# Three unused pieces of on-chip memory that move the start addresses of the weights, the features and the gated values

## The chip, the cores and the metric

The kernel runs on one core of a Trainium2 chip. The time is the device time of one execution in microseconds (us), the median of several runs. One run was also profiled. Everything is float32; the large products use the float32r kind of the matrix engine, with each operand split into a high and a low part.

## The reference, cut to what matters

Two transformer blocks over 512 tokens of width 1024 (528 tokens in the first block, with 16 meta tokens ahead):

```python
# first block, h is (528, 1024)
h = h + 0.5 * (silu(n1(h) @ w_gate1) * (n1(h) @ w_up1)) @ w_down1      # d_ff 2816
u = rmsnorm(h) ; parts = split(u @ w_in)                                # 20 + 16 blocks of 128 columns
y = sigmoid(g1) * (mla(parts) @ w_mla_o) + sigmoid(g2) * (gated_deltanet(parts) @ w_gdn_o)
h = h + y @ w_out
h = h + 0.5 * (silu(n2(h) @ w_gate2) * (n2(h) @ w_up2)) @ w_down2
x = rmsnorm(h)[16:]                                                     # (512, 1024)
# second block
shift, scale, gate = split(silu(c) @ w_ada + b_ada)
p = (rms_norm(x) * (1 + scale) + shift) @ w_in_2                        # q, k, v, gates
o = concat(banded_attention(p) * silu(z_a), (cmp + sel + win attention)(p) * silu(z_b))
out = x + gate * (o @ w_out_2)
```

## The kernel before

Everything lies transposed: 128 features on the partitions, tokens along the free dimension. A product sums over K blocks of 128 features. For each block the matrix engine (PE) makes three matmuls, because a product of split operands is high by high, high by low and low by high. The stationary operand (`lhsT`, loaded by a LDWEIGHTS that the profile shows as PEld) is a 128 by 128 piece of weights, and the moving operand (`rhs`) is a slice of features, 512 columns wide in most of the program and 272 and 256 columns (two halves of 528 tokens) in the first feed-forward layer and the projections after it. The loop that does most of it is in `mm_steps`, and its matmul is line 348:

```python
for a, x, first, last in ((wh, 0, c == 0, False), (wh, 1, False, False), (wl, 0, False, c == K - 1)):
    for i, (b, hl) in enumerate(zip(banks, xs)):
        T.matmul(b[:, :hl[x].shape[2]], lhsT=a[:, kk], rhs=hl[x][:, c], ...)
```

So the names of a row read like this: `b<-xh,whi` is a matmul into bank b with moving operand `xh` (features, high part) and stationary operand `whi` (weights, high part).

Weights come as raw pieces of 1024 columns (`wraw`) by DMA from SyncE's queue. `split_weights` halves each into two pieces of up to 512 columns, ScalarE (ACT, line 307) writes the high part and VectorE (DVE, line 308) the low part. A piece goes to one of three buffers `whi` and `wlo` in the pool `weights`, and every fourth piece to the extra buffers `whix` and `wlox`, which lie in a different pool at another place:

```python
more = extra[0] is not None and made[0] % (HALF + 1) == 0        # HALF = 3
hi, lo = [extra[0].tile([128, HW], F32R, tag=t + "x", ...) if more else
          wp.tile([128, HW], F32R, tag=t, ..., bufs=HALF) for t in ("whi", "wlo")]
```

A piece of 512 columns is four K blocks, so it feeds 12 matmuls of 512 moving columns, or 12 pairs of 272 and 256.

Pools are stacked from the left and from the right end of each partition's memory, tile after tile, in the order in which the program opens them. From the left stand first the pool `const` (the tiles `cst` of 2148 bytes and `vec` of 808 bytes), then `weights`, `big`, `small`, and then what a stage needs. From the right stand the features `xh0`, `xl0` (272 tokens) and `xh1`, `xl1` (256 tokens), later `xh2`, `xl2` and `h2`, and the three extra weight pools one after another (`weights_x1` in the first layer and the projections, `weights_x2` in the second feed-forward layer, `weights_x3`, from the left, in the second block's projections). So one small tile early in a pool shifts everything stacked behind it. The small tile `mod` (24 values, line 1345) stands at the bottom of the left side during the second feed-forward layer and the second block.

The program's stages, in order of time: the first feed-forward layer (`gh`, `gl` are its gated values), the input projections, the delta rule and latent attention (many small float32 matmuls, with projections woven in), the merge with the product `wo` (`mh`, `ml` are its moving operand), the second feed-forward layer, the second block's projections by tokens (`tok_group`, lines 1552 to 1554, in which features are the stationary and weights the moving operand), its attention, and the output product.

The order of the instructions is that of the program's text; generators are woven by hand with fixed rates (`weave`, `braid`), and nothing in it depends on an address.

Of the kernel before, what the change touches and what calls it, by code (L numbers as in the profile page):

```python
# [9 lines left out]
F32 = mybir.dt.float32  # L10
# [207 lines left out]
def body(tc, A, out, VAT, CAT):  # L218
# [4 lines left out]
    def pool(name, bufs=1, side="left", st=es, **k):  # L223
        return st.enter_context(tc.tile_pool(name=name, bufs=bufs, side=side, **k))
# [4 lines left out]
        return st  # L229

    const = pool("const")
    psum = pool("psum", 1, space=PSUM)
    dram = pool("dram", 1, space=DRAM)
    wp = pool("weights")
# [1107 lines left out]
    ast = scope()  # L1342
    apl = pool("ada", side="right", st=ast)
    mdp = pool("mod")
    mod = mdp.tile([128, 24], F32, name="mod")
    csil = apl.tile([128, D], F32, name="csil")
    ct = apl.tile([128, D], F32, tag="wada", name="ct", bufs=3)
    SY.dma_start(out=ct, in_=A["crow"])
# [641 lines left out]
```

## Time and profile before

| what | value |
|---|---|
| median of three runs | 1579.91 us (1579.36 to 1581.45) |
| time of the profiled execution | 1572.62 us |
| its span, first to last instruction | 1570.8 us |
| mean granted clock of PE | 0.998 |
| PE busy | 1540.9 us, 98% of the span, 10214 matmuls |
| VectorE busy | 995.9 us, 63% |
| ScalarE busy | 637.2 us, 41% |
| DMA | 178.69 MB, mean 114 GB/s |

The ends of matmuls are modelled and successive ones overlap, so the spacing of a stream of matmuls is read from the starts of its rows, not from the durations.

### The profile page before, as it was taken

The page shows a single profiled execution, that of the slowest core. Times are in us where ns is not written, and L with a number is a line of the kernel's source. Part 1 is how long each engine was busy: PE and PEld are TensorE (multiplying, and loading weights), DVE is VectorE, ACT ScalarE, POOL GpSimd, SP SyncE. Part 2 cuts the span into 40 slices and gives each one's busy share as a digit, 9 for nine tenths or more (in the row PEclk, how much of TensorE's full clock was granted, in tenths as well). Part 3 has the DMA queues.
Part 4 walks back from the last instruction along what each step waited for, and adds up shares of the span by engine and source line. Part 5 has one row for each costly group of instructions (what it writes and reads, how often), then busy time and mean ns, then how long its engine had stood idle before and what let it go on. Part 6 is the DMA issues. An engine that isn't in the chain of part 4 may idle for free.

```text
span 1570.8 us, 26635 instructions
## 1 busy us (share of the span) xinstructions
PE 1540.9 (98%) x10214; PEld 1347.4 (86%) x10214; DVE 995.9 (63%) x2338; ACT 637.2 (41%) x1303; POOL 167.3 (11%) x233
## 2 busy tenths in 40 slices
PE   8999999999999989998999999999999999999999
PEld 8999999999999888997777888888888978877667
DVE  6554345545788788656657697434554786669963
ACT  6332233334324333235554333323333564448741
POOL 0000000000001311012210000000000140125530
PEclk9999999999999999999999999999999999999999
DMA  5322333234424354325125584233332545522014
GB/s 179 94 93 74 100 96 95 91 88 129 137 83 125 105 152 130 106 83 180 35 81 165 201 276 136 80 99 106 95 91 81 150 140 176 175 84 53 11 37 139
DMA packets 94672, 178.69 MB, mean 114 GB/s; under 512 B 16608, under 2 KB 43808, under 8 KB 94544
## 3 DMA queue, kind: packets, MB, share of 16 engines
q1 hardware_dynamic: 93392, 174.89, 36.5%
q10 hardware_dynamic: 1152, 2.10, 0.4%
q8 instruction: 80, 1.31, 0.4%
q14 instruction: 48, 0.39, 0.1%
HBM read 159.80 MB, written 16.11 MB: 112 GB/s over the span
## 4 chain that ended last, share of the span: by engine, by line
PE 89%; DVE 5%; DMA 2%; POOL 1%; ACT 1%; issue 1%; SPq 0%; DVEq 0%; ACTq 0%; POOLq 0%
PE b L348 68%; PE b L1934 2%; PE b L1554 1%; PE b L1552 1%; PE b L1553 1%; PE b L521 1%; PE b L330 1%; PE b L1915 1%; PE b L332 1%; PE b L331 1%; PE b L1248 1%; PE b L1228 1%; DVE pr L960 1%; DVE wlo L308 1%; PE b L1838 1%
## 5 line engine op out<-in xcount | busy, mean ns | idle before, releaser
L307 ACT ACTIVATE whi<-wraw 128x512 fp32r<-128x512 f32 (+3 forms) x414 | 242.1, 587 | 484.6 <-PE b L348 433.0
L348 PE MATMUL b<-xh,whi 128*128 128x256 f32 (+2 forms) x1428 | 374.1, 319 | 0.4 <-DVE tv L372 0.4
L308 DVE TENSOR_TENSOR wlo<-wraw,whi 128x512 fp32r<-128x512 f32 (+3 forms) x414 | 263.5, 639 | 168.3 <-ACT whi L307 165.3
L348 PE MATMUL b<-xl,whi 128*128 128x256 f32 (+2 forms) x1428 | 369.4, 316 | 0.0
L348 PE MATMUL b<-xh,wlo 128*128 128x256 f32 (+2 forms) x1428 | 369.4, 316 | 0.0
L348 PEld LDWEIGHTS b<-xh,whi 128*128 128x128 f32 x1428 | 234.3, 189 | 21.3 <-issue 0.9
L348 PEld LDWEIGHTS b<-xh,wlo 128*128 128x128 f32 x1428 | 234.9, 189 | 18.8 <-issue 0.4
L348 PEld LDWEIGHTS b<-xl,whi 128*128 128x128 f32 x1428 | 234.4, 189 | 18.1 <-issue 0.4
L348 PE MATMUL b<-gh,wlo 128*128 128x256 f32 (+2 forms) x446 | 114.8, 310 | 0.0
L348 PE MATMUL b<-gh,whi 128*128 128x256 f32 (+2 forms) x446 | 114.8, 310 | 0.0
L348 PE MATMUL b<-gl,whi 128*128 128x256 f32 (+2 forms) x446 | 114.6, 309 | 0.0
L307 ACT ACTIVATE whix<-wraw 128x512 fp32r<-128x512 f32 (+4 forms) x109 | 61.8, 567 | 128.1 <-PE b L348 113.4
L308 DVE TENSOR_TENSOR wlox<-wraw,whix 128x512 fp32r<-128x512 f32 (+4 forms) x109 | 66.5, 610 | 53.3 <-ACT whix L307 53.0
L348 PE MATMUL b<-xh,whix 128*128 128x272 f32 (+2 forms) x308 | 82.5, 321 | 0.0
L348 PE MATMUL b<-xh,wlox 128*128 128x272 f32 (+2 forms) x308 | 81.7, 319 | 0.0
L348 PE MATMUL b<-xl,whix 128*128 128x272 f32 (+2 forms) x308 | 81.7, 318 | 0.0
L348 PEld LDWEIGHTS b<-gl,whi 128*128 128x128 f32 x446 | 73.8, 188 | 4.8
L348 PEld LDWEIGHTS b<-gh,wlo 128*128 128x128 f32 x446 | 73.8, 188 | 4.7
L348 PEld LDWEIGHTS b<-gh,whi 128*128 128x128 f32 x446 | 73.8, 188 | 4.8
L457 DVE TENSOR_TENSOR g<-b,R 128x272 f32<-128x272 f32 (+2 forms) x66 | 32.5, 516 | 61.1 <-PE b L348 58.7
L460 DVE TENSOR_TENSOR u<-b,R 128x272 f32<-128x272 f32 (+1 forms) x66 | 32.1, 515 | 59.7 <-PE b L348 59.7
L348 PEld LDWEIGHTS b<-xh,whix 128*128 128x128 f32 x308 | 51.0, 188 | 4.6 <-issue 0.5
(495 smaller groups left out, 2666.2 us busy)
## 6 DMA issues: line engine op xcount, KB each, us to landing
wraw<-in_wgu_dram SPq DMA_DIRECT2D x85, 512.0 KB, 3.6
wraw<-in_win_dram SPq DMA_DIRECT2D x36, 512.0 KB, 3.6
wraw<-in_wdn_dram SPq DMA_DIRECT2D x35, 384.0 KB, 3.5
wada<-in_wada_dram SPq DMA_DIRECT2D x24, 512.0 KB, 4.9
wraw<-in_wdn_dram SPq DMA_DIRECT2D x35, 320.0 KB, 2.9
wraw<-in_wo_dram SPq DMA_DIRECT2D x17, 512.0 KB, 3.6
wraw<-in_w2t_dram SPq DMA_DIRECT2D x16, 512.0 KB, 4.2
wraw<-in_w2f_dram SPq DMA_DIRECT2D x10, 512.0 KB
```

Source lines behind the costliest of these rows:

```text
L307: SC.activation(hi[:, :w], raw, AF.Copy)
L308: V.tensor_sub(lo[:, :w], raw, hi[:, :w].bitcast(F32))
L330: T.matmul(ps, lhsT=wh, rhs=xh, start=start, stop=False)
L331: T.matmul(ps, lhsT=wh, rhs=xl, start=False, stop=False)
L332: T.matmul(ps, lhsT=wl, rhs=xh, start=False, stop=stop)
L348: T.matmul(b[:, :hl[x].shape[2]], lhsT=a[:, kk], rhs=hl[x][:, c], start=first and not (one and i), stop=last and (i > 0 or not one))
L457: V.tensor_mul(g[:, o:o + w], b[:, :w], R[:, o:o + w])
L460: V.tensor_mul(u[:, o:o + w], b[:, :w], R[:, o:o + w])
L521: T.matmul(pp[2 * i + a][:, :n_], lhsT=w[j], rhs=X[a][x][:, k], start=first, stop=last)
L960: V.tensor_tensor(out=t, in0=x[:m, 0:i, 0:i], in1=g[:m, 0:i, i].unsqueeze(1).to_broadcast([m, i, i]), op=ALU.mult)
L1228: T.transpose(p[:, o:o + 128], d["pn"][par][:, i, NM + j * 128:NM + j * 128 + 128], ident)
L1934: T.matmul(po[rs[par], j * 128:], lhsT=vt[:, j, g * 64:g * 64 + 64], rhs=Pt[par][:, o:o + S - j * 128], start=False, stop=br == 1 and j == 3)
```

## The change

Three pieces are allocated that nothing reads or writes: 48 values (192 bytes) in the pool `const`, ahead of `cst` and `vec`; 56 values (224 bytes) at the right edge, ahead of every pool of the right side; and `mod` gets 32 places in place of 24 (32 bytes more), of which the first 24 are used.

```diff
     const = pool("const")
+
+    const.tile([128, 48], F32, name="pad")
+    pool("edge", side="right").tile([128, 56], F32, name="edge")
     psum = pool("psum", 1, space=PSUM)
...
     mdp = pool("mod")
-    mod = mdp.tile([128, 24], F32, name="mod")
+    mod = mdp.tile([128, 32], F32, name="mod")[:, 0:24]
```

On each of the five engines the same instructions stand in the same order, with the same shapes and the same waits; line numbers behind the edit are three higher. What differs is where tiles start. These are the starts in the built programs, in bytes of a partition, as the remainder of a division by 256:

| tiles | before | after |
|---|---|---|
| `wraw` (3), `whi` (3), `wlo` (3) | 64 | 0 |
| `whix`, `wlox` of `weights_x1` and `weights_x2` | 224 | 0 |
| `whix`, `wlox` of `weights_x3` | 32 | 0 |
| `xh0`, `xl0` (slices of 1088 bytes), `xh1`, `xl1` (1024 bytes) | 224 | 0 |
| `gh` / `gl` of the first layer (slices of 2112 bytes) | 64 / 0 | 0 / 192 |
| `gh`, `gl` of the second layer (2048 bytes) | 32 | 0 |
| `xh2`, `xl2`, `h2` (2048 bytes) | 224 | 0 |
| `mh`, `ml`, `ogh`, `ogl` (2048 bytes) | 64 | 0 |
| `wada`, `csil` | 224 | 0 |
| `hT` | 64 | 0 |
| `pna`, `pnb`, `xt` | 224 | 192 |
| `cst`, `accq` | 128 | 64 |

A K block of weights is 512 bytes and a slice of `xh2` 2048 bytes, so the remainder of a tile's start holds for all of its slices; only the slices of 1088 and 2112 bytes step on by 64 from one to the next.

## Rows read from the trace of the kernel before

**Rows 1.** The page's first part: busy time and share by engine.
```profile
PE 1540.9 (98%) x10214; PEld 1347.4 (86%) x10214; DVE 995.9 (63%) x2338; ACT 637.2 (41%) x1303; POOL 167.3 (11%) x233
```

**Rows 2.** The chain that ended last, by engine.
```profile
PE 89%; DVE 5%; DMA 2%; POOL 1%; ACT 1%; issue 1%; SPq 0%; DVEq 0%; ACTq 0%; POOLq 0%
```

**Rows 3.** Stretches: length, busy us (count) of PE, PEld, DVE, ACT, POOL; clock; DMA.
```profile
30.00:405.00 375.00, 375.00 (x3078) 374.78 (x3078) 188.61 (x359) 125.56 (x219) 2.63 (x9) 1.00 0.33 98
...
900.00:1250.00 350.00, 350.00 (x1591) 286.52 (x1590) 201.16 (x344) 122.91 (x216) 1.73 (x5) 1.00 0.40 123
1250.00:1420.00 170.00, 166.47 (x859) 136.88 (x858) 121.56 (x270) 88.50 (x192) 44.55 (x52) 1.00 0.48 147
```

**Rows 4.** PE's longest wait: us in total, times, longest.
```profile
PE b L521 <- ACT whi L307: 5.6, 1, 5.6
```

**Rows 5.** Groups of matmuls by line and shape: count, busy us, mean ns.
```profile
L348 PE MATMUL b<-xh,whi 128*128 128x256 f32 x704 | 175.3, 288 | 0.0
L348 PE MATMUL b<-xh,whi 128*128 128x512 f32 x388 | 154.6, 399 | 0.0
L348 PE MATMUL b<-xh,whi 128*128 128x272 f32 x336 | 97.6, 291 | 0.4 <-DVE tv L372 0.4
L348 PE MATMUL b<-gh,whi 128*128 128x512 f32 x104 | 41.1, 395 | 0.0
L1552 PE MATMUL b<-whi,xh 128*128 128x512 f32 x72 | 28.7, 401 | 0.0
```

**Rows 6.** Timeline of PE in the second feed-forward layer: start us, us.
```profile
943.07 0.40 PE L348 MATMUL b<-xh,whi 128*128 128x512 f32 x1
...
945.88 0.40 PE L348 MATMUL b<-xh,whix 128*128 128x512 f32 x1
...
946.81 0.39 PE L348 MATMUL b<-xl,whix 128*128 128x512 f32 x1
...
948.62 0.39 PE L348 MATMUL b<-xh,whi 128*128 128x512 f32 x1
```

**Rows 7.** Timeline of the weight loads beside the first of these matmuls.
```profile
943.07 0.19 PEld L348 LDWEIGHTS b<-xl,whi 128*128 128x128 f32 x1
```

**Rows 8.** Timeline of PE in the merge's product `wo`.
```profile
852.20 0.39 PE L348 MATMUL b<-mh,whi 128*128 128x512 f32 x1
...
854.93 0.39 PE L348 MATMUL b<-mh,whix 128*128 128x512 f32 x1
...
857.73 0.40 PE L348 MATMUL b<-mh,whi 128*128 128x512 f32 x1
```

**Rows 9.** Busy us of each engine during the two pieces of rows 6.
```profile
943.07:945.88 2.81, 2.81 (x13) 2.26 (x12) 2.81 (x6) 1.27 (x2) 0.00 (x0) 1.00 0.94 287
945.88:948.62 2.74, 2.74 (x13) 2.25 (x12) 2.74 (x5) 0.63 (x1) 0.00 (x0) 1.00 0.97 362
```

**Rows 10.** Timeline of PE in the second layer's down product.
```profile
1007.30 0.39 PE L348 MATMUL b<-gh,whi 128*128 128x512 f32 x1
...
1009.39 0.40 PE L348 MATMUL b<-gh,whi 128*128 128x512 f32 x1
```

**Rows 11.** Timeline of PE in `tok_group`, second block.
```profile
1322.25 0.39 PE L1552 MATMUL b<-whi,xh 128*128 128x512 f32 x1
...
1324.35 0.39 PE L1552 MATMUL b<-whi,xh 128*128 128x512 f32 x1
```

**Rows 12.** Timeline of PE in the first feed-forward layer, pairs of 272 and 256.
```profile
303.88 0.41 PE L348 MATMUL b<-xh,whi 128*128 128x272 f32 x2
...
306.81 0.40 PE L348 MATMUL b<-xh,whix 128*128 128x272 f32 x2
...
309.72 0.41 PE L348 MATMUL b<-xh,whi 128*128 128x272 f32 x2
```

**Rows 13.** Timeline of PE, a feature product with the third extra pool's weights.
```profile
1312.77 0.39 PE L348 MATMUL b<-xh,whix 128*128 128x512 f32 x1
...
1315.34 0.39 PE L348 MATMUL b<-xh,wlox 128*128 128x512 f32 x1
```

## The prediction

> **What bounds the kernel now.** I read the page's busy times first, then the chain, then single stretches, and last the starts of matmuls. PE is busy for 98% of the span [rows 1], and 89% of the chain that ended last is PE's own work [rows 2]. In the two long feed-forward stretches PE is busy for the whole of 375 and 350 us while VectorE is busy for 188.61 and 201.16 of them and ScalarE for less; in the second block's projections PE is busy for 166.47 of 170 us [rows 3]. Its longest wait for another engine is one of 5.6 us, for the first weights [rows 4]. So time comes or goes here with the spacing of matmuls in a stream that hardly waits. The granted clock is 1.00 in these stretches, which is the level of 2.4 GHz.
>
> The spacing is the thing to look at, since the change does nothing but move addresses. In the second feed-forward layer a piece of weights in `whi` and `wlo` starts at 943.07 and the next one, in `whix` and `wlox`, at 945.88: 2.81 us over 12 matmuls of 512 columns, 234.2 ns each. The piece in the extra buffers gets from 946.81 to 948.62 in its last eight: 1.81 over 8, 226 ns [rows 6]. Moving features, shapes and clock are the same; only the buffer differs. While one matmul streams, the load for the next one runs: the load that belongs to `xl,whi` starts at 943.07, at the start of the matmul of `xh,whi` [rows 6, 7]. By the table of addresses the features start at 224, `whix` at 224 too, `whi` at 64. The same comparison turned round stands in the product `wo`, where the moving `mh` starts at 64 as `whi` does: there the piece in `whi` takes 852.20 to 854.93, 2.73 over 12, 227.5 ns, and the piece in `whix` takes 2.80 over 12, 233.3 ns [rows 8]. So the cheaper buffer is the one that starts at the same remainder of 256 bytes as the moving operand, whichever that is. I read it as two reads, of the moving columns and of the next weights, that cost each other some 7 ns in 234 unless they run through memory in step. Two more pairs of tiles have this difference and are no better: `xh2` at 224 with `whix` of the third extra pool at 32 goes from 1312.77 to 1315.34 in 11 steps, 233.6 ns [rows 13], though 192 is a multiple of 64. Being in step by 256 is what I can point to.
>
> **The change part by part.** The two new pieces and the longer `mod` cost no instruction and no wait: each engine's instructions are the same as before in the same order. What they do is put `whi`, `wlo`, `whix`, `wlox` and the large moving tiles all at 0, so nearly every matmul of 512 columns has its pair in step. The sum, in parts:
>
> (a) `xh2` and `xl2` with `whi` and `wlo`: the row has 388 matmuls of high by high [rows 5], and each stands for three, 1164. They go from 234.2 to the level of matched pieces. That lies between 226 and 227.5 [rows 6, 8]; I take 227, so 7.2 ns and 8.4 us.
>
> (b) The second layer's gated values with `whi`, 32 against 64 now: 1007.30 to 1009.39 is nine matmuls, 232.2 ns [rows 10]. 104 by three is 312 [rows 5], 5.2 ns, 1.6 us.
>
> (c) The projections by tokens, where `whi` streams (64) and `xh2` is loaded (224): 1322.25 to 1324.35 is nine matmuls, 233.3 ns [rows 11]. 72 by three is 216 [rows 5], 6.3 ns, 1.4 us.
>
> (d) The pairs of 272 and 256 columns in the first layer and in the projections that need all 528 tokens. Slices of 1088 bytes step on by 64, so the 272 half can be in step with a quarter of its loads at most, before and after. The extra buffers start at 224 like `xh0` and `xh1`, so a piece in `whix` shows now what all pieces will be: 306.81 to 309.72, 2.91 over 12 pairs, 242.5 ns, against 2.93 over 12, 244.2 ns, for `whi` [rows 12]. 336 by three is 1008 pairs [rows 5], 1.7 ns each, 1.7 us.
>
> (e) Matmuls of 256 columns outside these pairs: 704 less 336 is 368, by three 1104 [rows 5]. No row shows them in step. If a pair gains as (d) does, one gains 0.85 ns, 0.9 us; at the other end nothing. Part of them is woven into the delta rule, where other engines set the pace too, so I take 0.5 us.
>
> This is 13.6 us. Pieces already in step (`whix` in the second layer, `whi` in `wo`) keep what they have. The down product of the first layer keeps the distance of its operands in `whi` (64 and 64 become 0 and 0, 0 and 64 become 192 and 0), so I count nothing. In the second block's projections PE is idle for 3.5 us of 170 [rows 3], and a part of what is won there will go into such waits; I take off 0.6 us. The forecast is 13.0 us less. VectorE and ScalarE, which make the weights, have cover: in a piece of 2.81 us ScalarE is busy for 1.27 us [rows 9], and over the second layer VectorE for 201 of 350 us [rows 3], so a piece that is 0.08 us shorter doesn't make either the bound.
>
> The profiled execution took 1572.62 us, which would become 1559.6. The median of the runs shown is 1579.91, 7.3 us above that execution; taking 13.0 us off it gives 1566.9 us, 0.8% less. A difference under 0.2%, about 3 us, I count as none.
>
> The bounds: at the upper end all matched pieces run at 226, another 1692 times 1 ns, 1.7 us, with (e) at 0.9 and no loss, which is 15.7 us and 1564.2. At the lower end, the first four matmuls of the matched piece in rows 6 take 0.93 us, 232.5 ns each; if the stream stayed at that, (a) would be 2.0, (c) 0.2 and (b) nothing, with (d) 1.7 about 4 us, and 1576.
>
> One rule of the Trainium skill speaks against all of this. The page "TensorE: Matmul & The Clock Gate", in its section "Step-by-step: what each phase is for", says that the matrix engine has two independent read ports into the on-chip memory, so that loading the next tile's weights doesn't take read bandwidth from the running matmul. By that rule the sum is nothing and the time stays at 1579.9. Rows 6 and 8 here differ by 6 to 8 ns with nothing but the tile of the load changed, which disagrees with it.
>
> **The rivals.** *Nothing happens.* The buffers differ for a reason other than addresses: the extra buffer is always the same one piece in four, and what ScalarE and VectorE do meanwhile repeats with the same period. For it: ScalarE is busy for 1.27 us during the piece in `whi` and 0.63 us during that in `whix` [rows 9]. Against it: in `wo` the same one in four is the slower one [rows 8], and `whix` of the third pool gains nothing [rows 13]. Time 1579.9. That two read ports don't disturb each other belongs here.
>
> *Half of it.* Part of the 7 ns is the access of ScalarE, which the piece in `whix` meets less, and part is address. Then (a) to (c) are worth half, 5.7 us, and with (d) 1.7 and (e) 0.5 less the 0.6 the sum is 7.3 us: 1572.6. Against it stands `wo`, where the difference is 5.8 ns the other way.
>
> *Slower.* With every tile at 0, the writes of VectorE and ScalarE into `whi` and `wlo` and their reads of `wraw` run in step with PE's reads too, and PE loses more to them than it wins. It decides from the point at which a matched matmul takes more than some 233 ns. If all 1692 of (a) to (c) went to 238 ns, so lost 4 to 6 where I let them win 5 to 7, that is 7.2 us more, 1587. Against it: in `wo` raw and split weights and the moving tile all start at 64 and the spacing is 227.5 [rows 8].
>
> *Much faster.* Zero itself matters, not only the distance: 512 columns at 2.4 GHz are 213.3 ns, and if the 1692 fell to that from 233.6, it would be 34 us, 1545. Against it: pairs in step at 64 [rows 8] and at 224 [rows 6] run alike, so the common start seems not to count.
>
> **How the numbers follow.** The forecast 0.73, nothing 0.07, half 0.12, slower 0.05, much faster 0.03. The predicted time is 1566.9. The range goes from 1563.5, which is the upper bound of the sum and the 0.6 us by which the lowest run lies under the median, to 1573.5, just beyond the half; it leaves out nothing, slower and much faster, 0.15. Faster by over 0.2% is the forecast, the half and the much faster case, 0.88; within it 0.07; slower 0.05.
>
> **What would show it.** If right, in the changed kernel's timeline the starts of `xh,whi` in the second layer are 226 to 228 ns apart, and `whi` and `whix` don't differ there or in `wo`; the rows of `gh` and of line 1552's successor are at 227 as well; pairs in the first layer are near 242.5; the durations of VectorE's and ScalarE's splits don't change; and PE's waits stay as short as now. If `whi` stays at 234 with the starts equal, the step from addresses to spacing is wrong. If the spacing falls as said and the time doesn't, the chain has another owner, which the waits would name. A spacing that falls in `wo` too, where the distance of `whi` doesn't change, would show that the common start counts.

## The result, and the profile after

The changed kernel takes 1559.85 us, the median of four runs (1557.84 to 1561.80), against 1579.63 us for the kernel before (1573.65 to 1581.45, four runs): a ratio of 0.9888, with an interval of 0.9841 to 0.9936. The prediction was 1566.9, with a range from 1563.5, so the time lies below the range. Of the four runs of the kernel before, three are those of the prediction's table (1579.36 to 1581.45); the one that was not known then took 1573.65. The profiled executions tell another part of it: 1572.62 us before, 1561.09 after, 11.5 us less, where the sum said 13.0.

The page's busy times and the chain by engine have hardly changed in shape; PE's busy time fell from 1540.9 to 1529.2 us [rows 1], with as many matmuls.

```profile
PE 1529.2 (98%) x10214; PEld 1348.4 (86%) x10214; DVE 995.7 (64%) x2338; ACT 636.0 (41%) x1303; POOL 167.1 (11%) x233
...
PE 88%; DVE 6%; DMA 3%; ACT 1%; POOL 1%; issue 1%; SPq 0%; DVEq 0%; ACTq 0%; POOLq 0%
```

The stretches (length, busy us and count of PE, PEld, DVE, ACT, POOL; clock; DMA): in the 350 us from 900 on, most of them the second feed-forward layer, 1645 matmuls start where there were 1591 [rows 3], with the same granted clock and VectorE and ScalarE far from full. Most of the 54 more are of 256 columns and come from the end of the layer, which now falls into this stretch, so the count doesn't give the gain. PE waits hardly more than before: in the second block's projections it is busy for 165.76 of 170 us, where it was for 166.47 [rows 3].

```profile
900.00:1250.00 350.00, 350.00 (x1645) 293.62 (x1643) 208.17 (x366) 129.44 (x234) 6.17 (x11) 1.00 0.42 128
1250.00:1420.00 170.00, 165.76 (x893) 137.63 (x892) 122.47 (x295) 89.56 (x203) 44.71 (x58) 1.00 0.45 139
```

PE's longest wait is still the one for the first weights, 5.5 us [rows 4].

```profile
PE b L524 <- ACT whi L310: 5.5, 1, 5.5
```

The spacing is where the time came from. PE's timeline (start us, us, row), five places in order of time: pairs of the first layer, the product `wo`, features with weights in the second layer, its down product, and the projections by tokens.

```profile
303.52 0.41 PE L351 MATMUL b<-xh,whi 128*128 128x272 f32 x2
...
306.44 0.41 PE L351 MATMUL b<-xh,whix 128*128 128x272 f32 x2
...
309.36 0.41 PE L351 MATMUL b<-xh,whi 128*128 128x272 f32 x2
...
852.16 0.39 PE L351 MATMUL b<-mh,whi 128*128 128x512 f32 x1
...
854.88 0.39 PE L351 MATMUL b<-mh,whix 128*128 128x512 f32 x1
...
856.92 0.39 PE L351 MATMUL b<-mh,whix 128*128 128x512 f32 x1
...
919.41 0.39 PE L351 MATMUL b<-xh,whi 128*128 128x512 f32 x1
...
922.13 0.39 PE L351 MATMUL b<-xh,whix 128*128 128x512 f32 x1
...
924.85 0.39 PE L351 MATMUL b<-xh,whi 128*128 128x512 f32 x1
...
1003.73 0.39 PE L351 MATMUL b<-gh,whi 128*128 128x512 f32 x1
...
1005.77 0.39 PE L351 MATMUL b<-gh,whi 128*128 128x512 f32 x1
...
1319.57 0.39 PE L1555 MATMUL b<-whi,xh 128*128 128x512 f32 x1
...
1321.61 0.39 PE L1555 MATMUL b<-whi,xh 128*128 128x512 f32 x1
```

In the second layer a piece in `whi` and one in `whix` now both take 2.72 us over 12 matmuls, 226.7 ns, where `whi` took 234.2 [rows 6]. In `wo` the two take 2.72 over 12 and 2.04 over 9, 226.7 both, where `whix` took 233.3 [rows 8]. The down product and the token projections are 2.04 over 9, 226.7 too, from 232.2 and 233.3 [rows 10, 11]. The pairs of the first layer are 2.92 over 12, 243.3 ns, in `whi` and in `whix` [rows 12]: no better on the whole.

To size each part I added up, over the two traces, the time from the start of each matmul to the start of the next, by the moving and the stationary tile (whichever stream they stand in; pairs are two matmuls; the differences are of unrounded sums):

| matmuls | count | before, us | after, us | difference | the prediction's term |
|---|---|---|---|---|---|
| 512 columns, `xh2`/`xl2` with `whi`/`wlo` | 1164 | 273.7 | 265.5 | -8.2 | (a) -8.4 |
| 512, second layer's `gh`/`gl` with `whi`/`wlo` | 312 | 72.7 | 70.7 | -2.0 | (b) -1.6 |
| 512, token projections with `whi`/`wlo` | 216 | 53.3 | 52.3 | -1.0 | (c) -1.4 |
| 512, the same three moving tiles with `whix`/`wlox` | 489 | 114.8 | 113.7 | -1.0 | not counted |
| 512, `ogh`/`ogl` | 192 | 47.8 | 46.2 | -1.6 | not counted |
| 512, `mh`/`ml` (waits for `mh` are in it) | 192 | 45.5 | 46.1 | +0.6 | nothing |
| 272 and 256 columns of the features and gated values | 5141 | 645.8 | 647.3 | +1.6 | (d), (e) -2.2 |

The first four rows come out the same, within 0.1 us, in every further trace of either kernel below. The last three don't: `ogh`/`ogl` are 46.6 in the second trace of the kernel before, so 0.3 us of the 1.6 is left; `mh`/`ml` are 45.9 there, and 45.7 and 45.6 in two more traces of the changed kernel; and the last row is 652.3 in the second trace of the kernel before, and 644.8 and 644.9 in those two of the changed kernel. So its +1.6 belongs to one execution and not to the change.

### The profile page after: what moved, and what is told of

It reads as the page before. It is cut to its first block, busy times and chain, and to the rows that moved or that the text cites. A ratio compares the mean times of both kernels' runs of the same rounds, so it can differ in the third digit from the quotient of the medians.

```text
span 1559.3 us, 26635 instructions
## 1 busy us (share of the span) xinstructions
PE 1529.2 (98%) x10214; PEld 1348.4 (86%) x10214; DVE 995.7 (64%) x2338; ACT 636.0 (41%) x1303; POOL 167.1 (11%) x233
## 4 chain that ended last, share of the span: by engine, by line
PE 88%; DVE 6%; DMA 3%; ACT 1%; POOL 1%; issue 1%; SPq 0%; DVEq 0%; ACTq 0%; POOLq 0%
PE b L351 67%; PE b L1937 2%; PE b L524 1%; PE b L1557 1%; PE b L1555 1%; PE b L1556 1%; PE b L1918 1%; PE b L333 1%; PE b L335 1%; PE b L334 1%; DVE wlo L311 1%; PE b L1251 1%; DVE pr L963 1%; DMA ta<-thD 1%; PE b L928 1%
```

## The experiments

The timed experiments ran in three batches, on two chips, each with the kernel before beside them; its medians there were 1572.4, 1573.2 and 1573.6 us.

**The kernel before and the changed kernel again.** No edit.

> The kernel before, once more, with a second trace. If the 7.3 us between its profiled execution and its median are scatter from one execution to the next, the new profile lies anywhere from 1572 to 1582 us and the spacing of matmuls is the same as in the first trace (234 ns for xh2 with whi, 227 for whix); if the spacing itself varies from one execution to the next, it shows here.

> The changed kernel, once more, against the kernel before in five rounds. Theory of the spacing alone: 11.5 us less (the difference of the two profiled executions), a ratio of 0.9927. Rival, that something else gains some 8 us which the two profiles don't show: 19 to 20 us less, a ratio of 0.9875.

The kernel before, run again as a kernel of its own: 1575.96 us (1574.14 to 1590.95), against 1572.43 of itself (11 runs), ratio 1.0038 (1.0002 to 1.0074), so a ratio made of four runs of one kernel can be off by some 0.4%. The changed kernel: 1560.54 us (1556.54 to 1561.81), ratio 0.9915 (0.9898 to 0.9932), 11.9 us. The gain here is that of the two profiles, not the 19.8 us of the two medians above.

The longest of these runs of the kernel before, 1590.95 us, was the profiled one. Its matmuls in the second layer stand as far apart as before: 2.81 us over 12, 234.2 ns [rows 6].

```profile
938.98 0.40 PE L348 MATMUL b<-xh,whi 128*128 128x512 f32 x1
...
941.79 0.40 PE L348 MATMUL b<-xh,whix 128*128 128x512 f32 x1
```

The time went elsewhere, into the delta rule. Windows there, first of this execution, then of the one profiled at the start (columns as above):

```profile
550.00:585.00 35.00, 31.49 (x249) 28.99 (x247) 31.27 (x93) 11.09 (x22) 7.42 (x6) 0.85 0.63 178
585.00:619.00 34.00, 34.00 (x204) 30.49 (x203) 15.26 (x37) 5.13 (x11) 0.00 (x0) 0.50 0.23 59
```

```profile
550.00:585.00 35.00, 30.42 (x291) 27.75 (x292) 31.45 (x96) 12.12 (x25) 7.00 (x6) 1.00 0.56 165
585.00:619.00 34.00, 33.44 (x332) 29.99 (x333) 26.94 (x77) 10.63 (x22) 5.28 (x4) 1.00 0.41 113
```

For 34 us the granted clock was 0.50, the lower of its two levels (1.2 GHz), and PE started 204 matmuls where it had started 332. In the 35 us before that PE had been idle for 3.5 us in this execution, and the mean clock was 0.85 already; in the other it had been idle for 4.6 us at 1.00, and the clock didn't fall there. Over the whole program behind its first 100 us, PE was at the lower level for 54.6 us in this execution and for 6.8 us in the first; in the changed kernel's first trace it was for 10.2 us. Each run's result gives its mean granted clock, and the times of both kernels go with it: of the kernel before 1568.1 us at 0.999, 1571.2 to 1574.8 at 0.996, 1578.9 and 1582.1 at 0.990, 1580.7 at 0.989, 1590.95 at 0.983, 1592.2 at 0.982; of the changed kernel 1556.5 at 0.999, 1558.0 to 1561.8 at 0.997, 1568.2 at 0.989, 1576.5 at 0.985.

**One end alone.** The left side's pieces (`pad` and `mod`) without the right side's, and the right side's without the left side's (edits against the changed kernel):

```diff
     const.tile([128, 48], F32, name="pad")
-    pool("edge", side="right").tile([128, 56], F32, name="edge")
```

> The piece in const and the longer mod alone: weights and gated values at 0, features still at 224. If the distance of the moving operand and the next weights counts, xh2 with whi stands at 224 in place of 160, which the second layer's gated values had before at 232 to 233 ns, so the second layer's gate and up products stay at 233 ns for whi and 227 for whix, and the time falls by 1 to 2 us at most. If a start at a multiple of 256 counts by itself, half of what is read is there and the time falls by 5 to 7 us.

```diff
-    const.tile([128, 48], F32, name="pad")
     pool("edge", side="right").tile([128, 56], F32, name="edge")
...
-    mod = mdp.tile([128, 32], F32, name="mod")[:, 0:24]
+    mod = mdp.tile([128, 24], F32, name="mod")
```

> The piece at the right edge alone: features and the extra weights at 0, other weights still at 64. If the distance counts, xh2 with whi stands at 192, which the third extra pool had before at 233 ns, and the projections by tokens go from 96 to 64, which was 229 ns with whix: the time falls by 1 to 2 us. The sum of this run's gain and that of the other half alone is then far less than the gain of both together. If a multiple of 256 counts by itself: 5 to 7 us less.

Left alone: 1569.65 us (1568.44 to 1572.19), ratio 0.9979 (0.9960 to 0.9998). Right alone: 1570.55 us (1569.83 to 1571.78), ratio 0.9983 (0.9965 to 1.0002). Together they are worth 11.9 us in the same batch, apart 2.8 and 1.9, which are both within the 0.4% that the ratio of one kernel to itself was off. The rows say more. With the left alone, the second layer's features (224) still don't match `whi` (now 0): from 936.61 to 944.30 are 33 matmuls, 233.0 ns. But `gh` and `whi` are both at 0 now, and from 1006.85 to 1010.26 are 15, 227.3 ns; in return `gh` with `whix` (224) went to 2.10 over 9, 233.3.

```profile
936.61 0.39 PE L350 MATMUL b<-xh,whi 128*128 128x512 f32 x1
...
944.30 0.40 PE L350 MATMUL b<-xh,whi 128*128 128x512 f32 x1
...
1006.85 0.39 PE L350 MATMUL b<-gh,whi 128*128 128x512 f32 x1
...
1010.26 0.40 PE L350 MATMUL b<-gh,whix 128*128 128x512 f32 x1
...
1012.36 0.39 PE L350 MATMUL b<-gh,whi 128*128 128x512 f32 x1
```

With the right alone, features and `whix` are both at 0 and `whi` is still at 64: `whix` takes 1.36 us over 6, 226.7 ns, and `whi` 7.00 over 30, 233.3.

```profile
935.98 0.39 PE L350 MATMUL b<-xh,whix 128*128 128x512 f32 x1
...
937.34 0.40 PE L350 MATMUL b<-xh,whi 128*128 128x512 f32 x1
...
944.34 0.40 PE L350 MATMUL b<-xh,whi 128*128 128x512 f32 x1
```

So neither the place of the weights nor that of the features gives the spacing by itself; their distance does.

**All at 32 instead of 0.** The two pads change sizes, so all these tiles start 32 bytes past a multiple of 256:

```diff
-    const.tile([128, 48], F32, name="pad")
-    pool("edge", side="right").tile([128, 56], F32, name="edge")
+    const.tile([128, 56], F32, name="pad")
+    pool("edge", side="right").tile([128, 48], F32, name="edge")
```

> Pads of 56 and 48 values in place of 48 and 56, so that weights, features and gated values all start at 32 past a multiple of 256. If only the distance between the moving operand and the next weights counts, every matmul of 512 columns stays at 227 ns and the time is that of the changed kernel, 11 to 13 us under the kernel before (a ratio of 0.991 to 0.993). If multiples of 256 count by themselves, the 512s go to 233 ns and the time to that of the kernel before.

The time is 1561.57 us, 0.9914 of before (0.9880 to 0.9947), as the changed kernel's; eight of its runs took 1558.67 to 1567.54 us, and one took 8464 us at a clock of 1.00; one of the kernel before beside it took 1773.83 us at 0.796. I have no explanation for either, and the ratio leaves them out. From 936.14 to 944.30 are 36 matmuls, 226.7 ns.

```profile
936.14 0.39 PE L351 MATMUL b<-xh,whi 128*128 128x512 f32 x1
...
944.30 0.39 PE L351 MATMUL b<-xh,whix 128*128 128x512 f32 x1
```

Zero has no virtue of its own. The change puts all of them at multiples of 256, but what counts is that the tiles start alike.

**PE alone.** A kernel that computes nothing of the reference: 48 matmuls each at eight distances of the moving tile `M` from the weights `W` (0, 32, ... 224 bytes, banks `da` to `dh`), first with the other engines idle, then with VectorE adding and ScalarE copying most of the time.

```diff
+STEPS = [0, 32, 64, 96, 128, 160, 192, 224]
+N_MM = 48
...
+            for i, d in enumerate(STEPS):
+                p = ps.tile([128, 512], F32, tag=f"b{i}", name="d" + "abcdefgh"[i])
+                for n in range(N_MM):
+                    k = n % 8
+                    T.matmul(p[:, 0:w], lhsT=W[:, k * 128:k * 128 + 128], rhs=M[:, d // 4 + k * 512:d // 4 + k * 512 + w],
...
```

> PE alone, with no other engine at work: streams of 48 matmuls whose moving operand starts 0, 32, ... 224 bytes (names da to dh) past the weights, modulo 256, for 128, 256, 272, 280 and 512 columns, then pairs of 272 and 256 with slices of 1088 bytes (ea to eh) and of 1280 bytes (fa to fh), then 256 and 512 again while VectorE and ScalarE copy. It computes none of the reference; its time means nothing. If PE's two reads disturb each other by their distance: 512 columns take 227 ns at distance 0, about 229 at 64 and 233 to 234 at 32, 96, 160, 192 and 224, with and without the copies. If the copies make the difference, all distances take the same 227 ns or less while PE is alone. For 280 columns distance 0 should be slower than 96 (133 against 129 ns), and the pairs about 242 to 244 ns at every distance with slices of 1088; whether slices of 1280 do better is open.

Its timeline, a row for each 48 matmuls: 512 columns and then 256 with the other engines idle, and 512 with both busy.

```profile
426.43 11.08 PE L39 MATMUL da<-M,W 128*128 128x512 f32 x48
437.35 11.37 PE L39 MATMUL db<-M,W 128*128 128x512 f32 x48
448.56 11.16 PE L39 MATMUL dc<-M,W 128*128 128x512 f32 x48
459.56 11.37 PE L39 MATMUL dd<-M,W 128*128 128x512 f32 x48
...
515.59 5.91 PE L39 MATMUL da<-M,W 128*128 128x256 f32 x48
521.33 5.82 PE L39 MATMUL db<-M,W 128*128 128x256 f32 x48
526.99 5.82 PE L39 MATMUL dc<-M,W 128*128 128x256 f32 x48
...
561.12 11.09 PE L39 MATMUL da<-M,W 128*128 128x512 f32 x48
572.05 11.37 PE L39 MATMUL db<-M,W 128*128 128x512 f32 x48
```

From row to row, divided by 48: 512 columns take 227.5 ns at distance 0, 233.5 at 32, 229.2 at 64, and over the five distances from 96 to 224 a mean of 233.5 (459.56 to 515.59, 240 matmuls). With VectorE and ScalarE busy (83.53 and 73.36 of 89.16 us) distance 0 takes 10.93 over 48, 227.7. For 256 columns the order is another: 119.6 at 0 and 117.9 at 32 and 64, but 119.6 at 96 too (532.65 to 538.39). For 280 columns I had expected 0 to be slower than 96, as in the kernel; it wasn't, with 127.9 ns (190.37 to 196.51) against 128.5 (208.73 to 214.90), a miss. For 512 columns this settles the two rivals that put part of the 7 ns on ScalarE: no other engine is needed for it, and VectorE and ScalarE add nothing to it. Each distance has its own bank in this run, so the bank changes with it; in the kernel the two pieces of rows 6 are halves of one product and go into the same bank. The rule that the prediction weighed, from the Trainium skill's page "TensorE: Matmul & The Clock Gate", section "Step-by-step: what each phase is for" (loading the next weights takes no read bandwidth from the running matmul), is not borne out by this stream: the loads are the same in all these rows, and where the moving operand starts against them alone moves the matmuls by 6 ns. That the two reads get in each other's way is the reading that fits; no run has the matmuls without the loads, so it is not shown.

**Pairs.** PE alone again, pairs of 272 and 256 columns at all 64 combinations of starts, and pairs of 264 and 264 at eight starts:

```diff
+                for t, o, w in ((p[0], d0 // 4 + k * slice0, w0), (p[1], 2368 + d1 // 4 + k % 6 * slice1, w1)):
+                    T.matmul(t[:, 0:w], lhsT=W[:, k * 128:k * 128 + 128], rhs=M[:, o:o + w], start=n == 0, stop=n == N_MM - 1)
```

> PE alone again: pairs of 272 columns (slices of 1088 bytes) and 256 columns (slices of 1024), 48 pairs for each of the 64 combinations of their starts, 0 to 224 bytes past the weights in steps of 32 (first letter of a name the 272, second the 256, a is 0, h is 224); then 264 and 264 with slices of 1056 (hi to hp). It computes none of the reference; its time means nothing. The pairs with equal starts (aa, bb, ..., hh) repeat 243.2 to 244.4 ns. If the 272 half is what costs, because its slices step on by 64, all combinations lie within 1 ns of that; if a combination is found at 240 ns or less, 1008 pairs of the first layer and its projections would give 3 us more.

All 64 lie between 243.0 and 245.5 ns a pair; the first two, a row for 96 matmuls:

```profile
27.26 11.84 PE L43 MATMUL aa<-M,W 128*128 128x272 f32 x96
38.94 11.87 PE L43 MATMUL ab<-M,W 128*128 128x272 f32 x96
```

11.68 us over 48 pairs is 243.3 ns. None of these placements helps the pairs. Pairs of 264 lie between 242.7 and 245.2 ns. The 240.6 ns that I read for the last of them (`hp`), and on which the next run was built, was a mistake: no row begins behind it, and I divided the 11.55 us from the start of its first matmul to the start of its last by 48 pairs, where they are 95 matmuls, 47.5 pairs: 243.1 ns.

```profile
858.67 11.83 PE L43 MATMUL hp<-M,W 128*128 128x264 f32 x96
```

What did help stands in the first run of PE alone, where pairs of 272 and 256 were also tried with slices of 1280 bytes for the 272, so that these too keep their remainder of 256: three of its eight starts took 240.0 to 240.2 ns, the others 243.3 to 246.5. One of the three:

```profile
344.89 11.69 PE L55 MATMUL fb<-M,W 128*128 128x272 f32 x96
356.41 11.85 PE L55 MATMUL fc<-M,W 128*128 128x272 f32 x96
```

**Halves of 264.** An attempt at a faster version on the strength of that 240.6: the 528 tokens in two equal halves, the second pair of halves cut to fit, and two more pads.

```diff
-HALVES = [(0, 272), (272, 256)]
+HALVES = [(0, 264), (264, 264)]
...
-    HF_ = [(0, 256), (256, 256)]
+    HF_ = [(0, 248), (248, 264)]
```

> The changed kernel with halves of 264 and 264 tokens in place of 272 and 256 in the first layer and its projections, their features 224 bytes past a multiple of 256 and weights still at 0, the combination that took 240.6 ns a pair in the stream of PE alone (hp) where 272 and 256 take 243 to 245. If the stream of PE alone carries over, the pairs of the first layer's gate and up products and of the projections fall by 2.5 to 3 ns, 1008 pairs, so 2.5 to 3 us less than the changed kernel, if its down product, whose slices start elsewhere, doesn't give it back; 14 to 16 us less than the kernel before. If VectorE's and ScalarE's work on unequal slices or the down product takes it back, the time is that of the changed kernel.

A miss: 1615.40 us (1611.91 to 1625.03), 1.0266 of before (1.0236 to 1.0296). The pairs themselves are no faster: from 300.14 to 308.93 are 36, 244.2 ns.

```profile
300.14 0.41 PE L351 MATMUL b<-xh,whi 128*128 128x264 f32 x2
...
308.93 0.41 PE L351 MATMUL b<-xh,whix 128*128 128x264 f32 x2
```

What made it slower is in the delta rule and the work woven into it (2000 matmuls in the program's order, from the 4000th on, take 282 us where the changed kernel's take 228), in new waits of PE for VectorE, one of them 17.4 us, and in the clock: 0.84 from 530 to 720, with PE busy for 152.89 of 190 us. Waits between 530 and 760 (us in total, times, longest), and the window:

```profile
PE b L872 <- DVE cs L849: 21.6, 2, 17.4
```

```profile
530.00:720.00 190.00, 152.89 (x1326) 140.34 (x1326) 125.14 (x338) 46.51 (x93) 24.75 (x20) 0.84 0.33 94
```

Why VectorE is late there I didn't settle. The changed kernel itself ran beside it once more:

> The changed kernel again, beside the one with halves of 264 on the same chip: 11 to 13 us under the kernel before.

It took 1561.14 us (1557.96 to 1576.46, 12 runs), 0.9936 of before (0.9914 to 0.9958); the runs of over 1568 us had a mean clock of 0.989 and less. No timed run beat the changed kernel. The slices of 1280 bytes are a lead that no run tried in the kernel.

## Why the prediction was right and where it failed

**The mechanism was right.** The spacing of 512 columns goes with the distance of the moving operand from the next weights by the remainder of 256. It shows in the changed kernel, in the two half changes, with all at 32, and with PE alone. That it is the two reads that get in each other's way is argued. *Nothing* falls with the spacing of rows 6 and 8 now equal, *half* with the idle VectorE and ScalarE of the PE-alone kernel. *Slower* falls since a matched matmul takes 226.7 ns and not over 233, with ScalarE's and VectorE's splits taking what they took; and so does *much faster*: a common start at 0 and at 32 gives 226.7 ns alike. The rows of the split and of the 280 columns, first of before, then of after (busy us, mean ns):

```profile
L308 DVE TENSOR_TENSOR wlo<-wraw,whi 128x512 fp32r<-128x512 f32 x277 | 191.8, 694 | 82.9 <-ACT whi L307 80.4
...
L1554 PE MATMUL b<-whi,xl 128*128 128x280 f32 x24 | 7.0, 291 | 0.0
```

```profile
L311 DVE TENSOR_TENSOR wlo<-wraw,whi 128x512 fp32r<-128x512 f32 x277 | 191.8, 695 | 81.8 <-ACT whi L310 79.4
...
L1557 PE MATMUL b<-whi,xl 128*128 128x280 f32 x24 | 7.2, 298 | 0.0
```

**The terms.** (a) measured 8.2 for 8.4, (b) 2.0 for 1.6, (c) 1.0 for 1.4. (d) and (e) were the mis-sized terms: 2.2 us forecast, and hardly anything came. In the first layer and the projections up to the delta rule, where the clock is 1.00, these matmuls take 496.9 us before and 496.3 to 496.6 in three traces of the changed kernel (497.8 in the second trace of the kernel before); behind that, their sum goes with the clock from one execution to the next. The 1.7 ns of a pair came from one piece of rows 12 and was no effect of the address: the 64 placements of pairs on PE alone all lie within 2.5 ns of each other, and the starts of 0 (`aa`) and 224 (`hh`) are at 243.3 and 244.2. The 263 single matmuls of 256 columns ahead of the delta rule took 31.5 us before and 31.6 after, and the 198 of 256 columns with the second layer's `gh` and `gl` lost 0.5 us (23.5 to 24.0, in every trace). The 280 columns of the rows above lost 0.4 us; I had put that down to `whi` and `xl2` coming into step, but on PE alone 0 is no slower than 96 for them, so its cause is open. What made up for part of it was not in the sum: the pieces in `whix`, 1.0 us (third pool, [rows 13], from distance 192 to 0, and the second layer's `gh` from 64 to 0), and some 0.3 us of `ogh`/`ogl`.

**The step that failed** is "taking 13.0 us off it gives 1566.9", off the median of the runs shown. It took the 7.3 us between the profiled execution and that median for a constant of the kernel. It wasn't: the changed kernel's median lies 1.2 us below its own profiled execution, and the medians of the kernel before beside the experiments were 1572.4 to 1573.6 us, next to the 1572.62 of its profile. The sum made against the profile, 1559.6, was the number to forecast; the range, from 1563.5, had left no room for the 7.3 us to go. What such an excess can be is shown for one execution, that of 1590.95 us: the clock at 1.2 GHz for 34 us on end in the delta rule, with the matmul spacing elsewhere unchanged. But that all three runs before the prediction had it would be odd: of the 42 runs of this kernel beside the experiments five took more than 1578 us. That the three runs of 1579.36 to 1581.45 us were of this kind is argued from their size alone (three runs of 1578.9, 1580.7 and 1582.1 us had clocks of 0.989 and 0.990); they have neither a clock nor a chip on record. Why those three were so long, and what starts such a fall, stays open.

## What to carry to other kernels

In a stream of matmuls that never waits, compare the spacing of rows that differ in nothing but a buffer: a difference of 7 ns in 234 was worth 8 us here, and two pads of some 200 bytes a partition and one of 32 got it. Put the moving tiles and the weight buffers of wide products (512 columns of float32r here) at the same remainder of 256 bytes, whichever; narrower ones (256 or 280 columns here) gain nothing or lose a little. And make the sum and the forecast from the same execution: when a median lies 0.5% from the profile, look at the granted clock of each run before carrying the difference along.

## What the hardware showed that was not expected

- A distance of 64 bytes is nearly as good as 0 (229.2 against 227.5 ns), but 192, the same distance the other way round, is not: 233.6 ns in [rows 13], and within the mean of 233.5 on PE alone.
- 512 columns in step take 226.7 ns at a granted clock of 1.00; no placement tried went lower.
- The time is PE's own: with VectorE and ScalarE at work beside it, 227.5 became 227.7 ns.
- 256 columns behave otherwise: 119.6 ns in step and at 96 bytes, 117.9 at 32 and at 64.
- Pairs of 272 and 256 columns stay within 243.0 and 245.5 ns wherever they start, as long as the slices of the 272 step by 1088 bytes; with 1280 the eight starts spread from 240.0 to 246.5.
